# Spacing attention heads evenly over the weight stream of a two-layer decoder

## The chip, the cores and the metric

The kernel runs on one core of one Trainium2 chip. The metric is the device time of one launch in microseconds (us); lower is better. All inputs are float32 in device memory, and the output has to agree with the reference in float32.

The engines that matter are TensorE (PE, matrix products; its weight loads are shown as PEld), VectorE (DVE), ScalarE (ACT), GpSimd (POOL) and SyncE (SP, which only issues transfers). Each has its own queue of instructions and works it off in order; semaphores make one engine wait for another.

## The reference

A batch of one sequence of 256 tokens, 2048 wide, goes through two layers. Layer 1 is a Mamba-2 mixer, layer 2 sparse latent attention with 32 heads, each followed by a residual and a layer norm. The change concerns layer 2 alone:

```python
c_q, c_kv, k_idx, w_idx, gate = split(x @ w_in)          # 512, 256, 64, 16, 4096 columns
c_q, c_kv = rms_norm(c_q), rms_norm(c_kv)
q      = c_q @ w_uq                                      # 32 heads of 128
q_lat  = einsum('bthd,hcd->bthc', q, w_uk)
sel    = top 64 keys of each token by the indexer's scores, causal
logits = einsum('bthc,btkc->bthk', q_lat, c_kv[sel]) * 128 ** -0.5
o_lat  = einsum('bthk,btkc->bthc', softmax(logits), c_kv[sel])
o      = einsum('bthc,hcv->bthv', o_lat, w_uv)
out    = (o * silu(gate)) @ w_out
x      = layer_norm(alpha * x + out)
```

The kernel computes keys and values of each head from `c_kv` with `w_uk` and `w_uv`, takes the logits over all 256 keys, and adds a mask made from the indexer's selection before the softmax. This gives the same numbers.

## The kernel before

All weights of both layers pass through the core once, as a **stream** of 404 units of up to 128 x 1024 numbers. For each unit SP loads it (line 99) into one of four `raw` buffers, ACT rounds it to `hi` (line 121), DVE takes the rest, `lo = raw - hi` (line 145), and PE multiplies both parts with the activations, so that a product of float32 numbers is made of three products of rounded ones. `hi` and `lo` have four buffers each. `Stream.run` goes through the units in order: it converts up to four units ahead (`convert_to`), issues the unit's matmuls (`pe`), and then takes **one step of every side task** that is active, oldest first. A side task is a Python generator; each `yield` ends its step. So the order of the instructions on every engine follows from the unit at which a task is started (`st.side(i, ...)`) and from its count of `yield`s. Below, a **block** is one unit with the side steps behind it.

In layer 2, after the latent projections and the indexer, come 16 **pairs** of heads. Pair p has these units:

- `pair_a(p)`: keys (`k`, lines 995 to 997) and values (`v`, lines 1004 to 1006) of two heads, 24 matmuls of 128x256
- `pair_b(p)`: queries (`q`, lines 1017 to 1019) of two heads, 24 such matmuls
- one gate (even p) or two gates (odd p) of two units each (`g`, line 337), 24 matmuls of 128x256 a unit; a gate's first unit has 16 with `hi` and then 8 with `lo`, its second 8 with `lo` and then 16 with `hi`

So an even pair takes four blocks, an odd one six, and two pairs ten blocks. `evac_steps` copies k, v and q out of PSUM (lines 1031 to 1046). Then `head_steps(h)` runs for each head, one step a block:

1. the **logits**: three 128x256 matmuls (lines 1055 to 1057) and one full float32 128x128 one (line 1058)
2. scale, mask and row extreme on DVE (line 1066)
3. exponentials on ACT (line 1071)
4. reciprocal and scaling on DVE (lines 1074, 1076), byte planes on POOL (line 1080), and a transposing transfer issued by SP (line 1082) from `cmask` to `ptu`, both single buffers
5. nothing
6. the planes are put together on POOL (line 1086)
7. the transposed probabilities are split into two parts, `prT` (ACT lines 1093 and 1094, DVE line 1095)
8. nothing
9. the **outputs**: three 128x256 matmuls (lines 1099 to 1101) and one float32 128x128 one (line 1102)
10. and three more steps multiply with the gate and split the result for the last projection (lines 1105, 1112, 1114)

Both heads of a pair use one task function; their starts are set by two lines:

```python
        st.side(i + 3, (head_steps, 2 * p))        # i is the unit of pair_b(p)
        st.side(i + 5, (head_steps, 2 * p + 1))
```

A logits or an outputs step puts four matmuls between two units' matmuls on PE; this is called a **visit** below. A visit is lone if its block has one of the two, and joint if it has outputs of an older head followed by logits of a newer one.

The columns of an answer of the timeline, as used below: start in us from the span's start, length in us, engine, line, operation, `out<-in` by the program's names, shape, how many in a row, and the idle time before it, if any.

Of the kernel before, what the change touches and what calls it, by code (L numbers as in the profile page):

```python
# [178 lines left out]
def trunk_kernel(ctx: ExitStack, tc: tile.TileContext, x, xt, w1, wdt, dtp, prm, wo1,  # L179
# [14 lines left out]
    st = Stream(nc, wraw, whi, wlo)  # L194
# [127 lines left out]
    def stream_w(half, cell, name):  # L322


        def pe(h, l):
            if half == 0:
                cell["ps"] = acc_tile(name)
            ps, xs = cell["ps"], cell["x"][0]
            first, second = (1, 0) if half else (0, 1)
            n, st.wide = T + st.wide, 0  # L330
            for lo in (first, second):
                for k in range(8):
                    kt = half * 8 + k
                    last = half == 1 and lo == second and k == 7
                    wt = (l if lo else h)[:, k * P:(k + 1) * P]
                    for c in (range(1) if lo else range(2)):
                        nc.tensor.matmul(ps[:, 0:n], wt, xs[:, kt, c * T:c * T + n],  # L337
                                         start=(kt == 0 and not lo and c == 0),
                                         stop=last and c == (1 - lo), skip_group_check=True)
                        n = T  # L340
        return pe
# [261 lines left out]
    for g in range(NG):  # L603
        for kind, n in (("B", 1), ("C", 1), ("x", 4), ("z", 4)):
            for ci in range(n):
# [5 lines left out]
                for half in range(2):  # L611
                    k = len(st.units)
                    i = st.add(w1[k], 1024, stream_w(half, cell, f"acc{k}"), STILL)
# [173 lines left out]
    def stream_tok(kb, width, cell, name, held=None):  # L787

        def mm(kb, h, l, half):
            ps = cell["ps"][half][:, 0:width]  # L790
            for k in range(2):
                kt = kb * 2 + k
                ah = X1[0][:, kt, half * P:(half + 1) * P]
                al = X1[0][:, kt, T + half * P:T + (half + 1) * P]
                hs, ls = (w[:, k * 512:(k + 1) * 512] if width == 512 else w[:, k, :]
                          for w in (h, l))
                nc.tensor.matmul(ps, ah, hs, start=(kt == 0), stop=False)
                nc.tensor.matmul(ps, ah, ls, start=False, stop=False)
                nc.tensor.matmul(ps, al, hs, start=False, stop=(kt == 15))

        def pe(h, l):
            if kb == 0:
                cell["ps"] = [acc_tile(f"{name}{j}") for j in range(2)]
            mm(kb, h, l, 0)
            if held is None:
                mm(kb, h, l, 1)
                return
            held.append((kb, h, l))
            L["early"](kb)
            if len(held) == EARLY:  # L810
                for a in held:
                    mm(*a, 1)
                st.limit = 1 << 30
                st.convert_to(n_o1 + EARLY + 4)
        return pe
# [95 lines left out]
    for kb in range(8):  # L911
        i = st.add(wcq[kb], 1024, stream_tok(kb, 512, cells["q"], "qp",
                                             held if kb < EARLY else None), MOVING)
    st.side(i, (lat_norm, cells["q"], 512, PC_QG, 4, "q", "cqT"))
    for kb in range(8):
        i = st.add(wkv[kb], 672, stream_tok(kb, 336, cells["kv"], "kvp"), TWO)
# [8 lines left out]
    def idx_pe(q, cell):  # L925
        def pe(h, l):
            cell["ps"] = acc_tile(f"ix{q}")
            for k in range(2):
                ps = cell["ps"][:, k * T:(k + 1) * T]
                for kt in range(4):  # L930
                    o = (k * 4 + kt) * P
                    nc.tensor.matmul(ps, h[:, o:o + P], cqT[:, kt, 0:T], start=(kt == 0), stop=False)
                    nc.tensor.matmul(ps, h[:, o:o + P], cqT[:, kt, T:2 * T], start=False, stop=False)
                    nc.tensor.matmul(ps, l[:, o:o + P], cqT[:, kt, 0:T], start=False, stop=(kt == 3))
        return pe
# [41 lines left out]
    for q in range(4):  # L977
        cell = {}
        i = st.add(wix[q], 1024, idx_pe(q, cell), STILL)
# [70 lines left out]
    def head_steps(h):  # L1050
        p, k = divmod(h, 2)
        (qh, ql, q1), (kh, kl, k1) = ([a[:, k, :] for a in PR[p][nm]] for nm in "qk")
        vh, vl, v2 = (a[:, k * P:(k + 1) * P] for a in PR[p]["v"])
        pl = y_tile(f"lg{h}")
        nc.tensor.matmul(pl[:, 128:384], qh, kh, start=True, stop=False)
        nc.tensor.matmul(pl[:, 128:384], qh, kl, start=False, stop=False)
        nc.tensor.matmul(pl[:, 128:384], ql, kh, start=False, stop=True)
        nc.tensor.matmul(pl[:, 0:128], q1, k1, start=True, stop=True)
        yield
        lg = d2.tile([P, 384], F32, tag="lg", name=f"lgs{h}")  # L1060
        mx = d2.tile([P, 2], F32, tag="mx", name=f"mx{h}")
        sm = d2.tile([P, 2], F32, tag="sm", name=f"sm{h}")
        rn = d2.tile([P, 2], F32, tag="rn", name=f"rn{h}")
        parts = ((0, 0, 128), (1, 128, 384))
        for j, a, b in parts:
            v.tensor_tensor_reduce(out=lg[:, a:b], in0=pl[:, a:b], in1=mb[:, a:b],
                                   scale=-ATT_SCALE, scalar=3.0e38, op0=ALU.add, op1=ALU.min,
                                   accum_out=mx[:, j:j + 1])
        yield
        for j, a, b in parts:  # L1070
            nc.scalar.activation(lg[:, a:b], lg[:, a:b], AF.Exp, scale=-1.0,
                                 bias=mx[:, j:j + 1], accum_out=sm[:, j:j + 1])
        yield
        v.reciprocal(rn, sm)
        for j, a, b in parts:
            v.tensor_scalar(lg[:, a:b], lg[:, a:b], rn[:, j:j + 1], 0.5,
                            op0=ALU.mult, op1=ALU.mult)
        halves = cmask.bitcast(U16)
        turned = d2.tile([P, 768], U16, tag="ptu", name=f"ptu{h}", bufs=1)
        nc.gpsimd.tensor_copy(halves.rearrange("p (a t) -> p a t", a=2),  # L1080
                              lg.bitcast(U16).rearrange("p (t a) -> p a t", a=2))
        nc.sync.dma_start_transpose(turned.rearrange("p (k t) -> p k t", k=6), halves)
        yield
        yield
        pt = d2.tile([P, 384], F32, tag="ptf", name=f"ptf{h}", bufs=1)
        nc.gpsimd.tensor_copy(pt.bitcast(U16).rearrange("p (t a) -> p a t", a=2),  # L1086
                              turned.rearrange("p (a t) -> p a t", a=2))
        yield
        if h == 0:
            d2.tile([P, 48], F32, tag="gap3", name="gap3", bufs=1)  # L1090
        ph, pl = (d2.tile([P, T], F32R, tag=f"prT{j}", name=f"prT{h}_{j}") for j in range(2))
        p2 = par[:, P * k:P * (k + 1)]
        nc.scalar.activation(ph, pt[:, 0:T], AF.Copy)
        nc.scalar.activation(p2, pt[:, T:384], AF.Copy)
        v.tensor_sub(pl, pt[:, 0:T], ph.bitcast(F32))
        yield
        yield
        po = m_tile(f"o{h}")
        nc.tensor.matmul(po[:, 0:T], vh, ph, start=True, stop=False)
        nc.tensor.matmul(po[:, 0:T], vh, pl, start=False, stop=False)  # L1100
        nc.tensor.matmul(po[:, 0:T], vl, ph, start=False, stop=False)
        nc.tensor.matmul(po[:, P:T], v2, p2, start=False, stop=True)
        yield
        og = d2.tile([P, T], F32, tag="og", name=f"og{h}", bufs=1)
        v.tensor_mul(og, po[:, 0:T], GT.pop(h))
        if h == 0:
            OG.append(big.tile([P, KT, 2 * T], F32R, tag="A", name="og0"))
        if h == 16:
            OG.append(big.tile([P, KT, 2 * T], F32R, tag="C", name="og1"))
        dst = OG[h // 16][:, h % 16, :]  # L1110
        yield
        nc.scalar.activation(dst[:, 0:T], og, AF.Copy)
        yield
        v.tensor_sub(dst[:, T:2 * T], og, dst[:, 0:T].bitcast(F32))
        yield
# [3 lines left out]
    for p in range(NH2 // 2):  # L1119
        src = wab[2 * p]  # L1120
        i = st.add(wab[2 * p], 1024, pair_a(p), KEYS)
        st.side(i, (evac_steps, p, ("k", "v")))
        i = st.add(wab[2 * p + 1], 1024, pair_b(p), STILL)
        st.side(i, (evac_steps, p, ("q",)))
        if p == 0:
            st.extra[i + 1] = 64
        st.side(i + 3, (head_steps, 2 * p))
        st.side(i + 5, (head_steps, 2 * p + 1))
        n = (left * (p + 1)) // 16 - (left * p) // 16
        for _ in range(n):  # L1130
            add_gate(next(gates))
# [366 lines left out]
```

## Time and profile before

| what | us |
|---|---|
| median of 3 runs | 1204.66 |
| the three runs | 1203.14, 1204.66, 1205.43 |
| the profiled run, device time | 1204.21 |
| its span, first to last instruction | 1202.5 |
| PE busy | 1195.6 |
| DVE busy | 926.5 |
| ACT busy | 679.9 |
| POOL busy | 183.9 |
| the 16 pairs, from the first k to the last gate | about 761.3 to 1015 |

The profile's page gives busy time and share of each engine, then the span in 40 slices, the DMA queues, the chain of work that ended last, and the costliest groups of instructions. A matmul's record is longer than the distance to the next one, since matmuls overlap; what one costs is read from the distance between starts. The granted TensorE clock was 1.000 over the whole span.

### The profile page before, as it was taken

The numbers are of one execution on the slowest core, as the hardware profiler recorded it, in microseconds if no ns is written. First come the engines' busy times: TensorE is split into PE (matmuls) and PEld (weight loads), VectorE is DVE, ScalarE is ACT, GpSimd is POOL, SyncE is SP. The second block draws the span as 40 slices with busy tenths as digits, with TensorE's granted clock in tenths as the row PEclk, the third lists the DMA queues.
The fourth block names the chain that finished last, engine by engine and source line by source line (L and its number), as shares of the span: only waits on it lengthen the run. The fifth ranks groups of instructions, "written<-read, shape, count | busy, mean of one in ns | idle before, by whom it ended". The sixth has DMA issues, their size and how long they took to land.

```text
span 1202.5 us, 22951 instructions
## 1 busy us (share of the span) xinstructions
PE 1195.6 (99%) x8817; PEld 1114.8 (93%) x8817; DVE 926.5 (77%) x1650; ACT 679.9 (57%) x1206; POOL 183.9 (15%) x211
## 2 busy tenths in 40 slices
PE   9999999999999999999999999999999999999998
PEld 8999999999999999788888899999999999888886
DVE  6888878888898888756556778878788888568467
ACT  6665666666666656544335656566766666443341
POOL 0112122112211210110000130032222222200000
PEclk9999999999999999999999999999999999999999
DMA  8676767677676765566666585666766667986662
GB/s 303 204 240 197 220 199 214 183 226 211 218 179 224 204 218 171 201 223 238 194 194 208 168 232 185 193 200 186 187 193 183 187 188 196 298 282 198 200 195 98
DMA packets 109757, 247.65 MB, mean 206 GB/s; under 512 B 52152, under 2 KB 52288, under 8 KB 109264
## 3 DMA queue, kind: packets, MB, share of 16 engines
q1 hardware_dynamic: 104736, 226.18, 62.0%
q0 software_dynamic: 4912, 20.02, 5.1%
q8 instruction: 69, 1.13, 0.4%
q14 instruction: 40, 0.33, 0.1%
HBM read 231.00 MB, written 4.28 MB: 196 GB/s over the span
## 4 chain that ended last, share of the span: by engine, by line
PE 96%; DVE 2%; ACT 1%; DMA 0%; issue 0%; SPq 0%; DVEq 0%; ACTq 0%
PE acc L337 33%; PE g L337 15%; PE o L637 10%; PE o L639 10%; PE o L638 10%; PE y L514 2%; PE q L1017 1%; PE q L1018 1%; PE q L1019 1%; PE acc_two L347 1%; DVE lo L145 1%; PE v L1004 1%; PE k L997 1%; PE v L1006 1%; PE k L996 1%; PE k L995 1%
## 5 line engine op out<-in xcount | busy, mean ns | idle before, releaser
L145 DVE TENSOR_TENSOR lo<-raw,hi 128x1024 fp32r<-128x1024 f32 (+1 forms) x400 | 490.2, 1228 | 217.5 <-ACT hi L121 217.0
L121 ACT ACTIVATE hi<-raw 128x1024 fp32r<-128x1024 f32 (+1 forms) x400 | 417.4, 1050 | 209.0 <-PE o L639 148.4
L337 PE MATMUL acc<-xT,hi 128*128 128x256 f32 (+1 forms) x2496 | 301.0, 277 | 0.0
L337 PEld LDWEIGHTS acc<-xT,hi 128*128 128x128 f32 x2496 | 291.1, 188 | 1.4 <-ACT E L449 0.9
L337 PE MATMUL acc<-xT,lo 128*128 128x256 f32 (+1 forms) x1248 | 156.5, 277 | 0.8 <-DVE lo L145 0.8
L337 PEld LDWEIGHTS acc<-xT,lo 128*128 128x128 f32 x1248 | 148.2, 188 | 2.3 <-DVE lo L145 1.2
L337 PE MATMUL g<-x1T,hi 128*128 128x256 f32 (+1 forms) x1024 | 124.8, 276 | 0.0
L337 PEld LDWEIGHTS g<-x1T,hi 128*128 128x128 f32 x1024 | 120.1, 188 | 0.2
L637 PE MATMUL o<-hi,yg 128*128 128x512 f32 x256 | 100.4, 392 | 0.1
L639 PE MATMUL o<-hi,yg 128*128 128x512 f32 x256 | 99.7, 389 | 0.0
L638 PE MATMUL o<-lo,yg 128*128 128x512 f32 x256 | 99.6, 389 | 0.0
L637 PE MATMUL o<-hi,og 128*128 128x512 f32 (+1 forms) x256 | 99.3, 388 | 0.0
L639 PE MATMUL o<-hi,og 128*128 128x512 f32 (+1 forms) x256 | 98.8, 386 | 0.0
L638 PE MATMUL o<-lo,og 128*128 128x512 f32 (+1 forms) x256 | 98.7, 386 | 0.0
L337 PE MATMUL g<-x1T,lo 128*128 128x256 f32 x512 | 69.9, 281 | 0.0
L397 DVE SCALAR_TENSOR_TENSOR ca<-acc,par,ca 128x255 f32<-128x255 f32 x138 | 66.1, 479 | 3.3
L337 PEld LDWEIGHTS g<-x1T,lo 128*128 128x128 f32 x512 | 62.7, 188 | 0.2
L404 ACT ACTIVATE xs<-ca 128x256 f32<-128x256 f32 x32 | 13.4, 419 | 84.2 <-DVE ca L397 50.4
L1086 POOL COPY ptf<-ptu 128x768 uint16<-128x768 uint16 x32 | 41.6, 1299 | 106.4 <-DMA ptu<-cmask 86.4
L637 PEld LDWEIGHTS o<-hi,yg 128*128 128x128 f32 x256 | 48.0, 188 | 10.5 <-DVE zs L415 0.5
L639 PEld LDWEIGHTS o<-hi,yg 128*128 128x128 f32 x256 | 48.1, 188 | 10.1
L638 PEld LDWEIGHTS o<-lo,yg 128*128 128x128 f32 x256 | 48.1, 188 | 9.8
(294 smaller groups left out, 1850.6 us busy)
## 6 DMA issues: line engine op xcount, KB each, us to landing
raw<-in_w_dram SPq DMA_DIRECT2D x160, 512.0 KB, 4.2
raw<-in_wo_dram SPq DMA_DIRECT2D x128, 512.0 KB, 4.2
raw<-in_wg_dram SPq DMA_DIRECT2D x64, 512.0 KB, 3.8
raw<-in_wab_dram SPq DMA_DIRECT2D x32, 512.0 KB, 3.8
abc<-acs_d POOLq DMA_DIRECT2D x32, 256.0 KB, 4.4
raw<-in_wcq_dram SPq DMA_DIRECT2D x8, 512.0 KB, 4.4
raw<-in_wkv_dram SPq DMA_DIRECT2D x8, 336.0 KB, 3.2
scr<-in_xt_dram SPq DMA_DIRECT2D x4, 512.0 KB, 6.3
```

The source lines that it names most:

```text
L121: self.nc.scalar.activation(h, r, AF.Copy)
L145: eng.tensor_sub(*self.halfway.pop(i))
L337: nc.tensor.matmul(ps[:, 0:n], wt, xs[:, kt, c * T:c * T + n], start=(kt == 0 and not lo and c == 0), stop=last and c == (1 - lo), skip_gr ...
L347: nc.tensor.matmul(cell["ps"][:, 0:n], w[:, k * P:(k + 1) * P], xcell[0][:, kt + j, c * T:c * T + n], start=first and j == 0, stop=last an ...
L397: v.scalar_tensor_tensor(acc[:, d:], ps[:, :T - d], w(k), acc[:, d:], op0=ALU.mult, op1=ALU.add)
L404: nc.scalar.activation(dst, acc, AF.Tanh)
L514: nc.tensor.matmul(py[ks, c * T + s * P:(c + 1) * T], xsT[:, s, c, ks], ms[c][k][:, ws], start=(c == 0 and s == 0), stop=(s == 1), skip_gr ...
L637: nc.tensor.matmul(ps, ah, hs, start=(kk == 2 * first), stop=False)
L638: nc.tensor.matmul(ps, ah, ls, start=False, stop=False)
L639: nc.tensor.matmul(ps, al, hs, start=False, stop=(kk == 31))
L995: nc.tensor.matmul(ps, h[:, 0, o:o + P], ckvT[:, ct, 0:T], start=(ct == 0), stop=False)
L1086: nc.gpsimd.tensor_copy(pt.bitcast(U16).rearrange("p (t a) -> p a t", a=2), turned.rearrange("p (a t) -> p a t", a=2))
```

## The change

Two edits in layer 2's heads. The first drops one of the two empty steps before the outputs for the first head of a pair (`k` is 0), so that its outputs come seven blocks behind its logits; the second head's stay eight behind. The second starts both heads of an odd pair one block later (`i + 4` and `i + 6` in place of `i + 3` and `i + 5`); even pairs start as before.

```diff
@@ -1094,7 +1094,8 @@
         nc.scalar.activation(p2, pt[:, T:384], AF.Copy)
         v.tensor_sub(pl, pt[:, 0:T], ph.bitcast(F32))
         yield
-        yield
+        if k:
+            yield
         po = m_tile(f"o{h}")
         nc.tensor.matmul(po[:, 0:T], vh, ph, start=True, stop=False)
         nc.tensor.matmul(po[:, 0:T], vh, pl, start=False, stop=False)
@@ -1124,8 +1125,8 @@
         st.side(i, (evac_steps, p, ("q",)))
         if p == 0:
             st.extra[i + 1] = 64
-        st.side(i + 3, (head_steps, 2 * p))
-        st.side(i + 5, (head_steps, 2 * p + 1))
+        for k in range(2):
+            st.side(i + (4 if p % 2 else 3) + 2 * k, (head_steps, 2 * p + k))
         n = (left * (p + 1)) // 16 - (left * p) // 16
         for _ in range(n):
             add_gate(next(gates))
```

Lines from the first edit on are one higher in the changed kernel (the outputs are lines 1100 to 1103 there). No instruction is added or taken away; they change places. Count the ten blocks of two pairs from 0, the `pair_a` unit of the even pair. Logits stood in blocks 4, 6, 8 and 0 and now stand in 4, 6, 9 and 1; outputs stood in blocks 2, 4, 6 and 8 and now stand in 1, 4, 6 and 9. Every outputs step now shares its block with another head's logits.

On PE around the start of an even pair, here pair 4 (`g13` is the second gate of pair 3, `o3`, `o4` outputs and `lg6`, `lg7` logits of those heads; the number in `hi280` is the unit). Before:

```order
L337 MATMUL g13_10079<-x1T_7955,hi279_9978 128x256 x16
L995 MATMUL k4_10172<-ckvT_8327,hi280_10027 128x256
...
L1006 MATMUL v4_10173<-hi280_10027,ckvT_8327 128x256
L1055 MATMUL lg7_10207<-hk3_0_9918,hq3_0_9972 128x256
...
L1058 MATMUL lg7_10207<-hk3_2_9920,hq3_2_9974 128x128
L1017 MATMUL q4_10230<-cqT_8325,hi281_10073 128x256
...
L1019 MATMUL q4_10230<-cqT_8325,lo281_10074 128x256
L337 MATMUL g14_10282<-x1T_7955,hi282_10118 128x256 x16
```

And with the change:

```order
L337 MATMUL g13_10079<-x1T_7955,hi279_9976 128x256 x16
L1100 MATMUL o3_10139<-prT3_0_10055,hv1_0_9461 128x256
...
L1058 MATMUL lg6_10152<-hk3_2_9916,hq3_2_9972 128x128
L995 MATMUL k4_10164<-ckvT_8327,hi280_10022 128x256
...
L1006 MATMUL v4_10165<-hi280_10022,ckvT_8327 128x256
L1017 MATMUL q4_10222<-cqT_8325,hi281_10073 128x256
...
L1019 MATMUL q4_10222<-cqT_8325,lo281_10074 128x256
L1100 MATMUL o4_10248<-prT4_0_10192,hv2_0_9720 128x256
...
L1058 MATMUL lg7_10257<-hk3_2_9916,hq3_2_9972 128x128
L337 MATMUL g14_10274<-x1T_7955,hi282_10108 128x256 x16
```

The lone logits visit between v and q is gone; a joint visit now stands before k and another behind q.

On SP in pairs 3 and 4 (`ptu2` is the transposing transfer of head 2, `raw278` the load of unit 278). Before:

```order
L1082 DMA_TRANSPOSE ptu1_9665<-cmask_95 128x6x128
L99 DMA raw277_9679<-in_wg_dram 128x1024
L99 DMA raw278_9737<-in_wg_dram 128x1024
L1082 DMA_TRANSPOSE ptu2_9769<-cmask_95 128x6x128
L99 DMA raw279_9788<-in_wg_dram 128x1024
L99 DMA raw280_9831<-in_wab_dram 128x1024
L1082 DMA_TRANSPOSE ptu3_9865<-cmask_95 128x6x128
```

And with the change:

```order
L1082 DMA_TRANSPOSE ptu1_9660<-cmask_95 128x6x128
L99 DMA raw277_9673<-in_wg_dram 128x1024
L99 DMA raw278_9730<-in_wg_dram 128x1024
L99 DMA raw279_9781<-in_wg_dram 128x1024
L1082 DMA_TRANSPOSE ptu2_9819<-cmask_95 128x6x128
L99 DMA raw280_9832<-in_wab_dram 128x1024
L99 DMA raw281_9866<-in_wab_dram 128x1024
L1082 DMA_TRANSPOSE ptu3_9905<-cmask_95 128x6x128
```

The transfers of an odd pair stand behind one load more; those of even pairs keep their places.

On DVE, around unit 281 with the change (`og` is an output times its gate, `lgs` the scaled logits):

```order
L145 TENSOR_TENSOR lo280_10023<-raw280_9832,hi280_10022 128x1024
L1115 TENSOR_TENSOR og0_9810<-og1_9957,og0_9810 128x256
L1106 TENSOR_TENSOR og2_10053<-o2_10008,sC_8087 128x256
L1095 TENSOR_TENSOR prT3_1_10056<-ptf3_10013,prT3_0_10055 128x256
L1074 RECIPROCAL rn4_9967<-sm4_9966 128x2
L1076 TENSOR_SCALAR lgs4_9964<-lgs4_9964,rn4_9967 128x128
...
L1066 ISA lgs5_10066,mx5_10067<-lg5_10017,mb_8328 128x128
...
L145 TENSOR_TENSOR lo281_10074<-raw281_9866,hi281_10073 128x1024
```

Before, the same block (block 7 of the ten) held all of these but line 1095, which stood one block earlier, behind `lo279`.

## The prediction

> **What bounds the kernel now.** I read the page first, then the waits of PE, then the waits of ACT in the heads' stage, and last the timeline block by block. From the page, the span, PE's row and the chain that ended last:
>
> ```profile
> span 1202.5 us, 22951 instructions
> PE 1195.6 (99%) x8817; PEld 1114.8 (93%) x8817; DVE 926.5 (77%) x1650; ACT 679.9 (57%) x1206; POOL 183.9 (15%) x211
> PE 96%; DVE 2%; ACT 1%; DMA 0%; issue 0%; SPq 0%; DVEq 0%; ACTq 0%
> ```
>
> PE holds 96% of the chain. Of 1202.5 us it lacks work for 6.9. Its waits, all of the run:
>
> ```profile
> PE zeros L728 <- DVE scr L723: 1.3, 1, 1.3
> PE acc L337 <- DVE lo L145: 0.8, 1, 0.8
> PE acc_two L347 <- ACT hi L108: 0.7, 1, 0.7
> ```
>
> None is in the heads' stage: no line of k, v, q, logits or outputs is there, and no gate. Two of the ten-block periods by windows (us, then busy us of PE, PEld, DVE, ACT, POOL):
>
> ```profile
> 834.84:866.91 32.07, 32.07 (x282) 32.07 (x281) 25.49 (x60) 21.48 (x53) 7.53 (x9) 1.00 0.73 186
> 866.91:898.98 32.07, 32.07 (x282) 32.07 (x281) 26.99 (x60) 21.48 (x53) 7.87 (x8) 1.00 0.71 187
> ```
>
> PE is busy through both to the last hundredth, and DVE has 5.1 to 6.6 us to spare in each. So a change of order can win nothing by ending a wait. It can win or lose in two ways only: through the distance at which PE starts one matmul after another, or through a new wait.
>
> **How far apart matmuls start.** PE's timeline has these rows for a gate, a k and v unit, and two q units. The first two rows and 844.25 below bound a gate's 24 matmuls; the next two bound a q unit with a logits visit before it (its first matmul, 0.20 us, is left out); then pair 0's q unit, which has no visit before it; then a k row.
>
> ```profile
> 841.53 1.98 PE L337 MATMUL g<-x1T,hi 128*128 128x256 f32 x16
> 843.35 1.07 PE L337 MATMUL g<-x1T,lo 128*128 128x256 f32 x8
> 858.26 0.28 PE L1018 MATMUL q<-cqT,hi 128*128 128x256 f32 x1
> 860.87 1.98 PE L337 MATMUL g<-x1T,hi 128*128 128x256 f32 x16
> 764.10 0.28 PE L1017 MATMUL q<-cqT,hi 128*128 128x256 f32 x1
> 766.92 2.02 PE L337 MATMUL g<-x1T,hi 128*128 128x320 f32 x16
> 866.91 0.28 PE L995 MATMUL k<-ckvT,hi 128*128 128x256 f32 x1
> ```
>
> The gate: 844.25 - 841.53 = 2.72 us for 24, 113.3 ns each. The q unit behind a visit: 2.61 us for 23, 113.5 ns. Pair 0's q unit: 2.82 for 24, 117.5 ns. k and v: 869.74 (below) - 866.91 = 2.83 for 24, 117.9 ns. The same 128x256 matmul thus has two spacings. The same q tensors show both, so it is not the operands alone: q is **fast** behind the float32 matmul of a visit, and **slow** where it follows slow v directly. k becomes slow when it follows a gate, and v stays so.
>
> [...]
>
> **What a visit costs.** Three rows for each kind: its start, the matmul behind it, and a later one. Lone logits between v and q, lone outputs within a gate, a joint visit within a gate, and a joint visit between v and q:
>
> ```profile
> 857.58 0.28 PE L1055 MATMUL lg<-hk,hq 128*128 128x256 f32 x1
> 858.06 0.37 PE L1017 MATMUL q<-cqT,hi 128*128 128x256 f32 x1
> ...
> 863.59 0.28 PE L1099 MATMUL o<-prT,hv 128*128 128x256 f32 x1
> 864.09 1.17 PE L337 MATMUL g<-x1T,lo 128*128 128x256 f32 x8
> 865.09 1.98 PE L337 MATMUL g<-x1T,hi 128*128 128x256 f32 x16
> ...
> 844.25 0.28 PE L1099 MATMUL o<-prT,hv 128*128 128x256 f32 x1
> 845.32 1.17 PE L337 MATMUL g<-x1T,lo 128*128 128x256 f32 x8
> 846.33 3.79 PE L337 MATMUL g<-x1T,hi 128*128 128x256 f32 x32
> ...
> 869.74 0.28 PE L1099 MATMUL o<-prT,hv 128*128 128x256 f32 x1
> 871.00 0.28 PE L1018 MATMUL q<-cqT,hi 128*128 128x256 f32 x1
> ```
>
> Each is taken to the point where the spacing is normal again, less the units' own matmuls at 113.3 ns. Lone logits: 858.26 - 857.58 - 0.113 = 0.57 us. Lone outputs: 1.50 - 8 x 0.113 = 0.59. Joint in a gate: 2.08 - 0.91 = 1.17. Joint between v and q: 1.26 - 0.11 = 1.15. A joint visit costs what two lone ones cost, 1.16, within 0.02. Every period trades one pair of lone visits for a joint one: eight times at most 0.02, under 0.2 us either way. I take **0**, the middle.
>
> **What changes in the spacing.** Seven even pairs (2, 4, ... 14) lose the visit between v and q and get one before k; pair 0 had none and stays. Odd pairs keep theirs.
> - q without a visit: if v ends slow, q stays slow, as pair 0's does: 24 x (117.5 - 113.4) = 0.10 us, seven times **+0.69**. If v ends fast, 0.
> - k behind a visit: the trace has no such place. Behind a visit q and gates run fast within four matmuls, which speaks for a fast k: 12 x 4.5 ns = 0.054 us, seven times **-0.38**. If k is slow whatever comes before it, 0.
> - v has operands of other roles (the latent is the stationary side, line 1004), so the stream changes between k and v as it does between a gate and k, where slow sets in. Fast v would be another -0.38. I take slow, by that nearest row.
>
> Sum: 0 + 0.69 - 0.38 = **+0.3 us**; bounds +0.7 (all slow) and -0.8 (all fast), a little over for the visits.
>
> **What could make PE wait.** The first head's outputs lose a block of slack. In pairs 5 and 6 the last part of the probabilities (DVE) and the outputs (PE) of a first head stand so:
>
> ```profile
> 869.77 0.41 DVE L1095 TENSOR_TENSOR prT<-ptf,prT 128x256 fp32r<-128x256 f32 x1
> 876.33 0.28 PE L1099 MATMUL o<-prT,hv 128*128 128x256 f32 x1
> 889.53 0.42 DVE L1095 TENSOR_TENSOR prT<-ptf,prT 128x256 fp32r<-128x256 f32 x1
> 895.67 0.28 PE L1099 MATMUL o<-prT,hv 128*128 128x256 f32 x1
> ```
>
> They are ready 6.15 and 5.72 us ahead. A block is 2.72 us bare and 3.89 with a joint visit, so at least 5.72 - 3.89 = 1.8 us stay. The cost is 0 while that cover holds.
>
> Blocks 2 and 7 now hold five kinds of DVE work. Block 7 before held four, and took this long:
>
> ```profile
> 851.84 1.23 DVE L145 TENSOR_TENSOR lo<-raw,hi 128x1024 fp32r<-128x1024 f32 x1 [0.57 <-ACT hi L121]
> 855.40 0.08 DVE L1066 DVE_READ_ACCUMULATOR2_ANT mx<- 128x1 f32 x1
> ```
>
> With line 1095 that is 3.64 + 0.33 = 4.0 us beside 2.72 of PE (no visit falls into these blocks): DVE ends 1.3 us late. What is queued behind it is the next `lo`. The tightest one once heads run, for a k unit:
>
> ```profile
> 860.25 1.23 DVE L145 TENSOR_TENSOR lo<-raw,hi 128x1024 fp32r<-128x1024 f32 x1 [0.47 <-ACT hi L121]
> 867.14 0.28 PE L997 MATMUL k<-ckvT,lo 128*128 128x256 f32 x1
> ```
>
> It is ready 867.14 - 861.48 = 5.7 us ahead, so 1.3 fits, and blocks 3 and 8 bring DVE little beyond the 1.23 of a `lo`. Cost 0.
>
> On SP an odd pair's transposes move behind one more load; SP then waits for POOL at another place, and loads behind it may be later. ACT's row in the heads' stage says how near that is:
>
> ```profile
> ACT hi L121 <- PE g L337: 0.2, 1, 0.2
> ```
>
> That is the only wait of a rounding in 254 us, and it is for PE, none for a load. Each load has four buffers of lead; two or three loads between transposes in place of two or four spread them more evenly. Cost 0. On POOL both copies of a head move with their transfer, past nothing but each other's; it is busy 7.5 of 32 us.
>
> **The rivals.**
> 1. All slow: k stays slow behind a visit, q becomes slow. For it: k and v are slow in every pair. Against it: every unit seen behind a visit is fast. Span + 0.69: 1205.35 on the median.
> 2. All fast: the visit before k carries through v and q. For it: fast persists from q to gates. Against it: the break between k and v. 0.76 less: 1203.9.
> 3. Spacing belongs to the tiles: k and v always slow, q fast but for pair 0. Then nothing changes: 1204.66. Against it: pair 0's q uses the same tensors.
> 4. Slower by a new wait: the first heads' outputs reach PE before their probabilities. It decides from 1.8 us of lateness in `prT`. DVE's 1.3 us must coincide with a late transpose; if both come to 2.5 us on all 16 first heads, 16 x (2.5 - 1.8) = 11 us: 1215.9. Against it: DVE's pile falls on the blocks after the first heads' line 1095, and the margin above is the lower bound.
>
> That the change does not do what it says I leave out: the order of instructions shows it done.
>
> **How the numbers follow.** The profiled run's span of 1202.5 becomes 1202.8, and with the 1.7 us around it (1204.21 - 1202.5) 1204.5 on the device. The profiled run was 0.45 under the median, so the median comes to 1204.66 + 0.3 = **1205.0**. Chances: the forecast 0.44, rival 1 0.24, rival 2 0.14, rival 3 0.09, rival 4 0.03, something not named 0.06. The first four lie between 1203.9 and 1205.35; the three runs shown lie 0.8 and 1.5 us to either side of their median; with some 1.4 us added at both ends the range is **1202.6 to 1206.8**, which leaves out rival 4 and most of the unnamed. About 0.2%, 2.4 us, is what a measurement of this kernel can tell from no change. None of the first four reaches it: same 0.91, faster 0.04, slower 0.05, the last from rival 4 and the unnamed.
>
> **What would show it.** In the changed profile: no wait of PE on `prT` or `lo` between 761 and 1015; pairs' periods of 32.07 + 0.04 us; q of pairs 2, 4, ... 14 taking 2.82 us for 24 matmuls (fast: 2.72); k of those pairs at 113 ns, v at 118; joint visits of 1.15 to 1.17. A period shorter by 0.1 would mean all fast. A PE row waiting for DVE line 1095 or ACT line 1093 would make the prediction wrong in kind; a span off by more than 2.4 us without such a row would mean that a cost outside the heads moved.

## The result and the profile after

| | before | changed |
|---|---|---|
| median, us | 1203.69 | 1211.36 |
| range of 6 runs each, us | 1203.13 to 1205.43 | 1210.39 to 1212.69 |
| the profiled run, us | 1204.21 | 1210.39 |
| its span, us | 1202.5 | 1208.7 |

The changed kernel takes 1.0062 times as long, with a 95% interval of 1.0051 to 1.0072. It is slower by more than the 0.2% that a measurement can tell, and the forecast of 1205.0 with its range up to 1206.8 was wrong.

The page's rows for the span, the busy times and the chain of the changed kernel:

```profile
span 1208.7 us, 22895 instructions
PE 1197.4 (99%) x8817; PEld 1116.2 (92%) x8817; DVE 930.8 (77%) x1650; ACT 683.4 (57%) x1206; POOL 187.3 (15%) x211
PE 96%; DMA 2%; DVE 1%; ACT 0%; POOL 0%; issue 0%; SPq 0%; POOLq 0%; DVEq 0%
```

PE's gap, span less busy, grew from 6.9 to 11.3 us, and transfers now hold 2% of the chain, where they held nothing. The longest of PE's waits over the whole run (us in total, times, longest) says what the new gap is:

```profile
PE o L1100 <- ACT prT L1093: 4.3, 1, 4.3
```

This row is new, the longest in the list, and a single wait. It lies at the outputs of head 31, the last head, after the pairs have ended. The windows of a whole period of the heads' stage (us, then busy us of PE, PEld, DVE, ACT and POOL, PE clock, DMA share, GB/s) show no gap there:

```profile
854.02:886.18 32.16, 32.16 (x284) 32.16 (x282) 27.13 (x59) 22.13 (x54) 10.09 (x9) 1.00 0.75 201
```

A period takes 32.16 us where it took 32.07. The same points of the program in the two profiled runs give a balance. The points are starts in PE's timeline, in us; line 637 is the last projection:

| point | before | changed | changed less before |
|---|---|---|---|
| first k of the pairs | 761.27 | 760.55 | -0.72 |
| 1st matmul of line 637 there | 1015.11 | 1014.82 | -0.29 |
| 41st | 1045.47 | 1050.34 | 4.87 |
| 61st | 1059.07 | 1065.25 | 6.18 |
| end of the span | 1202.5 | 1208.7 | 6.2 |

The pairs begin 0.72 us earlier in the changed run, and over them it loses 0.43. Between the 1st and the 41st matmul of line 637 it loses 5.16, between the 41st and the 61st another 1.31, and after that nothing. These sum to 6.18, the whole difference of the spans.

So the loss is one event of 6.47 us in the 50 us after 1015. POOL's queue shows how it comes about. In the timeline of POOL before, head 31's second copy (line 1086, behind its transposing transfer) stands ahead of two loads for the last layer norm, `fin<-x_d` and `fin<-in_lnr_dram` of 2 MB each:

```profile
1034.21 1.07 POOL L1086 COPY ptf<-ptu 128x768 uint16<-128x768 uint16 x1 [5.54 <-DMA ptu<-cmask]
1035.18 0.54 POOL L1392 DMA_DIRECT2D fin<-x_d  x1
1035.71 0.53 POOL L1394 DMA_DIRECT2D fin<-in_lnr_dram  x1
```

And with the change:

```profile
1031.50 1.69 POOL L1080 COPY cmask<-lgs 128x768 uint16<-128x768 uint16 x1 [1.01 <-DVE lgs L1076]
1033.13 0.54 POOL L1393 DMA_DIRECT2D fin<-x_d  x1
1033.67 0.53 POOL L1395 DMA_DIRECT2D fin<-in_lnr_dram  x1
1047.47 1.03 POOL L1086 COPY ptf<-ptu 128x768 uint16<-128x768 uint16 x1 [13.28 <-DMA ptu<-cmask]
```

The loads are written into the program behind the block of a fixed unit (line 1389 before, `st.run(n_heads + 6)`). Head 31 belongs to an odd pair, so its steps moved back one block. The second copy now falls behind the loads, and the loads are issued in the same microsecond as head 31's transposing transfer. That they meet is no chance: the loads follow head 31's first copy (line 1080) on POOL at once, and the transfer reads what the same copy writes. SP's timeline of the changed kernel has the transfer here:

```profile
1033.21 1.21 SPq L1082 DMA_TRANSPOSE ptu<-cmask  x1
```

The view of transfers for the issues from 1033 to 1034 us (KB, and us from issue to landing):

```profile
fin<-x_d POOLq DMA_DIRECT2D x1, 2048.0 KB, 8.5
fin<-in_lnr_dram POOLq DMA_DIRECT2D x1, 2048.0 KB, 13.0
ptu<-cmask SPq DMA_TRANSPOSE x1, 14.1
```

Before, the same transfer was issued at 1028.69 us, without them:

```profile
ptu<-cmask SPq DMA_TRANSPOSE x1, 5.4
```

It takes 14.1 us in place of 5.4. It lands at 1047.3, 0.6 us behind the second load (1033.67 + 13.0 = 1046.7). The Trainium skill ("DMA: Bandwidth & Descriptors", section "Issuing engines are not separate DMA queues") says that transfers issued by sync and by gpsimd run on the same 16 engines and interleave. The trace agrees in so far as a transfer of SP's queue is held up by loads of POOL's; that it lands behind all of them is what this trace adds.

PE starts head 31's outputs after a wait of 4.28 us:

```profile
1049.01 0.38 PE L1100 MATMUL o<-prT,hv 128*128 128x256 f32 x1 [4.28 <-ACT prT L1093]
```

The windows from there:

```profile
1049.00:1050.00 1.00, 0.92 (x3) 0.72 (x4) 0.41 (x1) 1.00 (x2) 1.00 (x2) 0.72 1.09 447
1050.00:1052.00 2.00, 2.00 (x8) 1.71 (x7) 1.84 (x2) 2.00 (x4) 0.55 (x2) 0.50 0.87 264
1052.00:1054.00 2.00, 2.00 (x8) 1.59 (x8) 2.00 (x4) 0.30 (x1) 0.00 (x0) 0.79 0.90 199
1054.00:1056.00 2.00, 2.00 (x11) 1.62 (x10) 0.71 (x3) 1.36 (x2) 0.00 (x0) 1.00 0.97 336
```

Behind the gap the granted clock falls to 0.50 and is back at 1.00 by 1054. Lost at that clock: 1 x 0.28 + 2 x 0.50 + 2 x 0.21 = 1.7 us. With the wait that is 6.0 of 6.47; the rest was not traced. The Trainium skill ("TensorE: Matmul & The Clock Gate", section "HAM oscillation — how this bites in real kernels") says that PE idle for more than about 3.4 us is throttled to half clock; the trace agrees, with a gap of 4.28 us and a clock of 0.50.

The profiled run is the fastest of the six. It and one more (1210.39 and 1210.43 us) have a mean granted clock of 0.999, the four others (1211.14 to 1212.69) one of 0.997. Half a clock over 3.4 us, as in the windows above, lowers the mean over 1209 us by 0.0014; 0.997 takes about twice that (an estimate from these numbers). So the median loses more than this trace shows, and the lower clock fits as the reason; those four runs have no trace.

### The profile page after: what moved, and what is told of

Same layout as the page of the kernel before. It is cut to its first block, busy times and chain, and to the rows that moved or that the text cites. A ratio compares the mean times of both kernels' runs of the same rounds, so it can differ in the third digit from the quotient of the medians.

```text
span 1208.7 us, 22895 instructions
## 1 busy us (share of the span) xinstructions
PE 1197.4 (99%) x8817; PEld 1116.2 (92%) x8817; DVE 930.8 (77%) x1650; ACT 683.4 (57%) x1206; POOL 187.3 (15%) x211
## 3 DMA queue, kind: packets, MB, share of 16 engines
HBM read 231.00 MB, written 4.28 MB: 195 GB/s over the span
## 4 chain that ended last, share of the span: by engine, by line
PE 96%; DMA 2%; DVE 1%; ACT 0%; POOL 0%; issue 0%; SPq 0%; POOLq 0%; DVEq 0%
PE acc L337 35%; PE g L337 15%; PE o L637 9%; PE o L638 9%; PE o L639 9%; PE y L514 2%; PE q L1017 1%; PE q L1018 1%; PE q L1019 1%; DMA ptu<-cmask 1%; DMA scr<-in_xt_dram 1%; PE v L1004 1%; PE k L997 1%; PE k L995 1%; PE k L996 1%; PE v L1006 1%
## 5 line engine op out<-in xcount | busy, mean ns | idle before, releaser
L145 DVE TENSOR_TENSOR lo<-raw,hi 128x1024 fp32r<-128x1024 f32 (+1 forms) x400 | 498.4, 1248 | 212.0 <-ACT hi L121 210.8
L337 PE MATMUL g<-x1T,lo 128*128 128x256 f32 x512 | 65.9, 278 | 0.0
L1086 POOL COPY ptf<-ptu 128x768 uint16<-128x768 uint16 x32 | 44.9, 1404 | 114.1 <-DMA ptu<-cmask 89.7
L637 PEld LDWEIGHTS o<-hi,yg 128*128 128x128 f32 x256 | 48.0, 188 | 10.3 <-DVE zs L415 0.3
L637 PEld LDWEIGHTS o<-hi,og 128*128 128x128 f32 x256 | 48.5, 189 | 9.7
L639 PEld LDWEIGHTS o<-hi,og 128*128 128x128 f32 x256 | 48.3, 189 | 9.8
```

Source lines behind the costliest of these rows:

```text
L145: eng.tensor_sub(*self.halfway.pop(i))
L637: nc.tensor.matmul(ps, ah, hs, start=(kk == 2 * first), stop=False)
L639: nc.tensor.matmul(ps, al, hs, start=False, stop=(kk == 31))
```

## The experiments

The theory behind all of them, called A: the loss is this one event, the two loads beside head 31's transfer, which brings the wait and, through the wait, the lower clock. The letters in the expectations: rival B is the first heads' shorter distance, C the order or the time of POOL's queue, D the loads slowing PE or its weights by themselves, E a cause of the later 1.3 us that is not the clock. Each ratio is against the kernel before, run on the same chip; its median was 1203.63 for the first four kernels, 1203.97 for the next four and 1204.02 for the last.

**Which edit?** The first experiment is the kernel before with seven blocks of distance for the first head of even pairs alone:

```diff
         v.tensor_sub(pl, pt[:, 0:T], ph.bitcast(F32))
         yield
-        yield
+        if h % 4:
+            yield
```

> The kernel before, with the outputs of the first head of even pairs alone seven blocks behind its logits; no start is moved, so head 31 and the last layer's loads keep their places. Theory A (the cost of the change is one event: head 31's transposing transfer is issued together with the two last-layer loads of 2 MB each and lands 14 us later in place of 5, so that PE waits 4.3 us for its outputs and then runs at half clock for about 2.5 us, which costs 1.3 us more): same as before, within 0.5 us, 1203.7; no PE wait in the heads' stage. Rival B (the first heads' shorter distance costs): slower by half of the change's cost, about 1207.

Measured: 1203.90 us (10 runs), ratio 1.0000 (0.9991 to 1.0010), and no wait of PE in the heads' stage. Seven blocks are enough there. The other half of the split is the changed kernel with the second edit alone:

```diff
-        if k:
-            yield
+        yield
```

> The changed kernel with both heads eight blocks behind, so only the odd pairs' start is moved. Theory A: head 31's place is all that counts, so this is as slow as the change: about 1211, one PE wait of 4 to 5 us on prT of head 31 near 1045. Rival B: near 1204 to 1205, since no distance is shorter.

Measured: 1210.93 us (4 runs), ratio 1.0067 (1.0052 to 1.0082), with the wait on top of PE's waits:

```profile
PE o L1099 <- ACT prT L1093: 4.0, 1, 4.0
```

The second edit alone does it. It does not touch the distance between logits and outputs, so a lack of slack there is not the cause. The first edit for all pairs without the second was not tried: outputs of neighbouring heads then fall into adjacent blocks, with a single `og` buffer between them.

**Is it the loads?** The changed kernel with the loads one block later, and the kernel before with the loads one block earlier:

```diff
-    st.run(n_heads + 6)
+    st.run(n_heads + 7)
```

> The changed kernel with the last layer's two loads (fin from x1_d and from the norm's weights) issued one block later, behind head 31's second POOL copy as before. Theory A: the transfer lands within 6 us, no PE wait, 1204.4: what is left over the kernel before is the slow spacing of q, six periods of 0.09 us, 0.5 us. Rival B: no change, 1211. Rival C (the cost is POOL's own time for issuing the loads ahead of the copy, 1.1 us): also about 1204, told apart from A by the half-bytes run.

```diff
-    st.run(n_heads + 6)
+    st.run(n_heads + 5)
```

> The kernel before with the same two loads issued one block earlier, ahead of head 31's second POOL copy. No head is moved. Theory A: the collision comes without the change: the transfer lands 12 to 14 us after its issue, PE waits 2 to 4 us for head 31's outputs: 1206 to 1210, and above 1207 only if the wait also lowers the clock. Rival B: 1203.7, no wait.

The loads later, in the changed kernel: 1204.19 us (10 runs), ratio 1.0005 (0.9995 to 1.0014). No wait for `prT` is left, and in POOL's timeline the copy has its data early:

```profile
1037.50 1.06 POOL L1086 COPY ptf<-ptu 128x768 uint16<-128x768 uint16 x1 [2.68 <-DMA ptu<-cmask]
```

The transfer itself, issued at 1034.84 us:

```profile
ptu<-cmask SPq DMA_TRANSPOSE x1, 2.5
```

The loads earlier, in the kernel before: 1210.48 us (4 runs), ratio 1.0054 (1.0039 to 1.0069). PE waits 4.1 us for `prT`. POOL's timeline:

```profile
1028.48 0.54 POOL L1392 DMA_DIRECT2D fin<-x_d  x1
...
1044.70 1.04 POOL L1086 COPY ptf<-ptu 128x768 uint16<-128x768 uint16 x1 [15.15 <-DMA ptu<-cmask]
```

And its transfers from 1028 to 1030 us:

```profile
ptu<-cmask SPq DMA_TRANSPOSE x1, 16.0
```

The same loss comes up in a kernel in which no head was moved, and goes from the one in which heads were. That settles the place and the partner of the collision.

**The order of POOL's queue, or the bytes?** One rival (C) was that the second copy is late because it stands behind the loads' issue on POOL. In this version of the changed kernel only the first load stays ahead of the copy; the second comes two blocks later:

```diff
     st.side(n_heads + 13, (x1_steps,))
+    st.run(n_heads + 8)
     nc.gpsimd.dma_start(gbf, lnr[2:4, :].rearrange("(o h) t -> o h t", o=1).broadcast_to([P, 2, D]))
```

> The changed kernel with the second of the two last-layer loads (the norm's weights) issued two blocks later; the first stays ahead of head 31's POOL copy, so half the bytes go beside the transfer. Theory A: the transfer lands about half as late, 7 to 9 us after its issue, which the eight blocks cover: no PE wait, 1204.4. Rival C (POOL's queue order, not the bytes): the wait stays, 1210 to 1211.

Measured: 1204.72 us (10 runs), ratio 1.0005 (0.9996 to 1.0014). POOL's timeline:

```profile
1033.74 0.54 POOL L1393 DMA_DIRECT2D fin<-x_d  x1
...
1043.30 1.05 POOL L1086 COPY ptf<-ptu 128x768 uint16<-128x768 uint16 x1 [9.02 <-DMA ptu<-cmask]
```

The transfers issued beside that load:

```profile
fin<-x_d POOLq DMA_DIRECT2D x1, 2048.0 KB, 8.6
ptu<-cmask SPq DMA_TRANSPOSE x1, 9.3
```

The copy still stands behind a load in POOL's queue, but with 2 MB the transfer takes 9.3 us in place of 14.1, and head 31's slack just covers that. What POOL waits for in all these rows is the transfer; the issue of a load takes it 0.54 us. So the loads in flight set the delay, not the order of POOL's queue. One load against two does not tell the bytes from the number of loads.

**What does the late transfer stop?** If only the outputs wait, then outputs two blocks later should be free of it:

```diff
         if k:
             yield
+        if h == 31:
+            yield
+            yield
         po = m_tile(f"o{h}")
```

> The changed kernel with head 31's outputs alone two blocks further behind (ten behind its logits). The loads and the transfer collide as in the changed kernel. Theory A: the transfer still lands 12 to 16 us after its issue, but two blocks of 3 us each cover the 4.3 us of wait: no PE wait, 1204.4. Rival D (the loads slow PE or the weights' loads themselves, and the wait only shows it): still about 1210.

Measured: 1210.39 us (4 runs), ratio 1.0049 (1.0033 to 1.0065). The expectation failed. PE's waits are now for weights:

```profile
PE o L637 <- ACT hi L121: 2.6, 1, 2.6
...
PE o L638 <- DVE lo L145: 0.8, 1, 0.8
```

ACT's timeline shows why:

```profile
1049.73 0.42 ACT L1093 ACTIVATE prT<-ptf 128x256 fp32r<-128x256 f32 x1 [11.34 <-POOL ptf L1086]
```

The outputs no longer wait, but ACT works in order and stands 11.34 us at the split of head 31's probabilities. Behind it stand the roundings of the next units, and PE runs out of weights 3.4 us long (2.6 + 0.8, with one matmul between). The clock falls here too, though no single gap is longer than 2.6 us: the windows 1052 to 1054, 1054 to 1056 and 1056 to 1058 have 0.71, 0.50 and 0.94, which lose 2 x 0.29 + 2 x 0.50 + 2 x 0.06 = 1.7 us. With the gaps that is 5.1 of the 6.5 by which this span is longer than before (1209.0 against 1202.5). The wait on line 1100 in the changed kernel was only the first place where this was felt. So the theory was refined: the split itself has to come later. The next version of the changed kernel puts it and all behind it back by four blocks, and leaves the loads where they are:

```diff
                               turned.rearrange("p (a t) -> p a t", a=2))
         yield
+        if h == 31:
+            for _ in range(4):
+                yield
```

> The changed kernel with head 31's split of the probabilities (ACT lines 1093 and 1094, DVE line 1095) and everything behind it four blocks later. The two last-layer loads are still issued beside head 31's transposing transfer, so that transfer should still land about 14 us after its issue. Theory A as it stands after the run that put only the outputs later (what costs is that ACT and DVE, in order, stand behind the late split and stop converting weights): four blocks are 10.9 us and the wait there was 11.3 us on ACT against 0.4 where nothing is late, so ACT should idle about 1 us or less at the split, PE should not wait for it nor for hi or lo behind it, its clock should stay at 1.00, and the time should be 1203.7 to 1205. Theory D (the loads themselves slow the weight stream or PE while they run): 1209.5 to 1211 as with the change, with PE waits for hi or lo whose own row names a DMA of raw.

Measured: 1205.31 us (10 runs), ratio 1.0009 (1.0000 to 1.0019). Its transfer is as late as with the change:

```profile
ptu<-cmask SPq DMA_TRANSPOSE x1, 13.9
```

PE's only wait between 1015 and 1070 us is 0.4 us, for a `lo` of line 145. ACT's timeline:

```profile
1049.81 3.47 ACT L121 ACTIVATE hi<-raw 128x1024 fp32r<-128x1024 f32 x3 [7.72 <-DMA raw<-in_wo_dram]
1053.17 0.40 ACT L1096 ACTIVATE prT<-ptf 128x256 fp32r<-128x256 f32 x1
```

Nearly the whole loss is gone: from the 1st to the 61st matmul of line 637 it takes 44.72 us, against 43.96 before and 50.43 with the change, so 0.76 of the 6.47 stay. So the lateness costs through ACT and DVE, which wait for it in order. The median is 0.3 us above the expected interval, and one part of the expectation missed: with the split out of the way, ACT idles 7.72 us for a weight load of SP's queue, and PE feels 0.4 us of it. Rival D, that the loads hold up the weight stream by themselves, therefore holds for 0.8 us at most and not for 6. ACT's wait of 7.72 us hardly reaches PE; that the lead of the weight buffers covers it is the likely reason, not one that a run isolates.

**Is the second part the clock?** In the changed kernel, 18 float32 128x128 matmuls of the identity, whose result nothing reads, fill PE's queue ahead of head 31's outputs:

```diff
         po = m_tile(f"o{h}")
+        if h == 31:
+            fill = s_tile("fill")
+            for _ in range(18):
+                nc.tensor.matmul(fill[:, 0:P], ident, ident, start=True, stop=True)
```

> The changed kernel with 18 float32 128x128 matmuls into an unused PSUM bank just ahead of head 31's outputs, about 4.2 us of work of no use that PE does where it would wait. Theory A with the clock as a cost of its own: the wait for prT shrinks to under 1 us, the clock stays at 1.0, and the 1.3 us of half clock are saved: 1210.0 on the median. Rival E (the 1.3 us behind the wait are not the clock's): 1211.4, as the change.

Measured: 1210.08 us (4 runs), ratio 1.0047 (1.0033 to 1.0061). PE's wait for `prT` is 0.3 us. The windows behind it:

```profile
1049.00:1051.00 2.00, 1.63 (x13) 1.24 (x11) 0.42 (x1) 1.15 (x3) 2.00 (x4) 1.00 1.04 424
1051.00:1053.00 2.00, 2.00 (x12) 1.69 (x12) 1.53 (x2) 2.00 (x4) 0.85 (x2) 1.00 1.00 301
```

The time of the wait is spent on the filler, and the clock stays at 1.00. The two steps of the balance, 5.16 and 1.31 us in the changed kernel, are 4.80 and 0.12 here, 1.55 less in all, near the 1.7 counted from the clock rows. All four runs have a mean clock of 0.999 or 1.000, where four of the changed kernel's six had 0.997. The ratios' intervals overlap, so the run times alone do not separate it; the trace and the clocks do.

**Does a longer matmul make k fast?** This one tests the prediction's reading of the rhythm. In the kernel before, the first k matmul of pairs 1 to 15 is made 320 columns wide; its extra 64 columns fall into the second head's half, which is computed afresh afterwards.

```diff
-                    nc.tensor.matmul(ps, h[:, 0, o:o + P], ckvT[:, ct, 0:T], start=(ct == 0), stop=False)
+                    w = 64 if p and k == 0 and ct == 0 else 0
+                    nc.tensor.matmul(pk[:, k * T:(k + 1) * T + w], h[:, 0, o:o + P], ckvT[:, ct, 0:T + w],
+                                     start=(ct == 0), stop=False, skip_group_check=True)
```

> The kernel before with the first matmul of each pair's k (pairs 1 to 15) 320 columns wide in place of 256; the 64 more columns are overwritten by the second key half. If the slow spacing is a state that a longer matmul ends, k and v run at 113 ns: 24 x 4.5 ns less 27 ns for the columns, 15 pairs, 1.2 us less: 1202.4. If the slow spacing belongs to k and v themselves, 0.4 us more: 1204.0.

Measured: 1204.45 us (11 runs), ratio 1.0005 (0.9997 to 1.0014). Its first two k rows of pair 6 and the first v row in PE's timeline:

```profile
854.61 0.31 PE L996 MATMUL k<-ckvT,hi 128*128 128x320 f32 x1
854.75 0.28 PE L998 MATMUL k<-ckvT,hi 128*128 128x256 f32 x1
...
856.05 0.28 PE L1008 MATMUL v<-hi,ckvT 128*128 128x256 f32 x1
```

From the second k matmul to v are 11 at (856.05 - 854.75) / 11 = 118 ns. k stays slow, and so does v; a first matmul of 320 columns does not make them fast.

No version among these beat the kernel before.

## Why the prediction was wrong

**The step that failed** is the one on the queues in "What could make PE wait": "On POOL both copies of a head move with their transfer, past nothing but each other's", and with it the cost of nothing that was put on the moved transposes ("On SP an odd pair's transposes move behind one more load ... Cost 0"). Both were read from the steady periods, and there they hold. For the last head they do not: its second copy moved past two loads of 2 MB, and its transfer came to stand beside them. The transfer took 14.1 us in place of 5.4, and ACT and PE waited for it. That cost 6.47 us in the trace; the medians differ by 7.67 (1211.36 - 1203.69), pairs and lower clocks included. It could be read beforehand: POOL's timeline before has the loads at 1035.18, 0.97 us behind the start of head 31's second copy at 1034.21, and their place in the code is tied to a unit, not to a head. A step moved by a block, 2.72 us or more, had to cross that. The price would have had to be bounded from the 4 MB; the window from 1040 to 1045 before, with the loads in flight, shows 424 GB/s:

```profile
1040.00:1045.00 5.00, 5.00 (x26) 4.19 (x25) 2.76 (x3) 2.08 (x3) 0.00 (x0) 1.00 1.00 424
```

4.19 MB at that rate are 9.9 us, an estimate; the transfer came 8.7 us later than before. Either is more than head 31's slack of 5.5 us before (its last `prT` part ended at 1036.6, its outputs began at 1042.12).

**The slack of the first heads.** "At least 1.8 us stay" was right. Of 16 first heads the least has 1.76 us between its last `prT` part and its outputs, and none waits. Rival 4, the only one with a new wait, named the wrong heads; even pairs alone at seven blocks measured 1.0000. Its sign came true by another mechanism, in the row that the prediction had named as "wrong in kind": a PE wait for ACT line 1093, yet outside the 761 to 1015 us in which it was looked for.

**DVE's pile.** Five kinds of work in one block cost PE nothing, as forecast: the period above has PE busy to the hundredth.

**The rhythm.** Forecast was +0.04 us a period, rival 1 (all slow) gave 0.10, and six periods measure +0.09: rival 1 is what the spacing does in six of the seven pairs. PE's timeline of the changed kernel, pair 4 behind a joint visit: the second k, the first v and q, and the outputs behind q.

```profile
822.06 0.28 PE L996 MATMUL k<-ckvT,hi 128*128 128x256 f32 x1
823.36 0.28 PE L1004 MATMUL v<-hi,ckvT 128*128 128x256 f32 x1
824.77 0.28 PE L1017 MATMUL q<-cqT,hi 128*128 128x256 f32 x1
827.60 0.28 PE L1100 MATMUL o<-prT,hv 128*128 128x256 f32 x1
```

q: 827.60 - 824.77 = 2.83 us for 24, slow as forecast. k: 1.30 us for 11, 118 ns, and here the forecast failed; "fast within four matmuls" was read from q and gates and does not carry to k. In pair 2, whose k follows a lone visit, the same points are

```profile
789.98 0.28 PE L996 MATMUL k<-ckvT,hi 128*128 128x256 f32 x1
791.24 0.28 PE L1004 MATMUL v<-hi,ckvT 128*128 128x256 f32 x1
792.60 0.28 PE L1017 MATMUL q<-cqT,hi 128*128 128x256 f32 x1
795.43 0.28 PE L1100 MATMUL o<-prT,hv 128*128 128x256 f32 x1
```

k at 1.26 / 11 = 115 and v at 1.36 / 12 = 113 ns are fast, and q is slow behind a fast v. So "if v ends fast, 0" for q was wrong too, and rival 3 (spacing belongs to the tiles) falls with rival 2. What decides between the two spacings was not found. The term came to +0.43 us over the pairs, against a forecast of +0.3. That the two are near is partly luck: q is slow in all seven pairs as counted (+0.69), but k and v are fast in one pair alone (24 x 4.5 ns, -0.11), not k in seven (-0.38), and the remaining -0.15 was not traced.

**The total.** Without the event the changed kernel would have come out near where the forecast put it: with the loads moved one block it takes 1204.19 us, 0.56 more than the kernel before beside it (1203.63), and by the interval no different from it.

## What to carry to other kernels

When steps shift by a constant, check the last instance as well as the steady one: what stands in each queue right behind it is often tied to something else, here a unit's number. A small transfer that several engines wait for in order should not be issued together with megabytes on another queue; here its delay grew with the loads in flight (9.3 us to landing beside 2 MB, 14.1 beside 4 MB), and it counts against the slack of everything queued behind its consumers. Here moving the large transfers behind the small one's landing (1204.19 us) served as well as, or better than, moving the small one's consumers (1205.31).

## What was unexpected in the hardware

- A transposing transfer of 128x768 two-byte numbers landed 2.5 and 5.4 us after its issue without the large loads, 9.3 beside 2 MB of them, and 13.9 to 16.0 beside 4 MB. Beside the loads it landed 0.6 to 0.8 us behind the last of them wherever this was read.
- One gap of 4.28 us on PE was followed by half a clock for 3.4 us, which cost about 1.6 us more; with a gap of 0.3 us the clock did not move. The half clock did not last equally long in all runs: with the second edit alone (a wait of 4.0 us) the windows of 2 us from 1047 to 1055 have 0.65, 0.50, 0.50 and 0.65, which is half a clock for 6.8 us.
- Matmuls of one shape keep to one of two spacings, 113 or 118 ns. With a lone visit before k, which one pair of the changed kernel has, k and v ran fast and the q after them slow; with a joint visit before k all three ran slow; a first k matmul 64 columns longer left both slow.
